# The middle outputs of a fast causal convolution, moved from VectorE to GpSimd

## The chip, the cores and the metric

The kernel runs on one core of a Trainium2 chip. The metric is the device time of one execution in microseconds (us); the kernel before takes 746.35 us, the median of two runs (746.24 and 746.46). The engines are TensorE (PE; PEld is its weight load), VectorE (DVE), ScalarE (ACT), GpSimd (POOL) and the queue engine SyncE (SP). Each runs its own list of instructions in order, and they wait for one another through semaphores.

## The reference

```python
# x: (8, 4096, 512) f32, kernel: (8, 512, 512) f32
out = zeros_like(x)
for k in range(8):
    # shifted: x moved k places later along the sequence, zeros ahead
    out += matmul(shifted(x, k), kernel[k])
```

It is a causal convolution along the sequence with 8 taps, and each tap is a 512 x 512 matrix.

## The kernel before

The 8 x 4096 positions are cut into 128 runs of 256 positions, one run to a partition row. Position t of all 128 runs is one block of 128 x 512. Of each run the first four positions (HEAD) are computed directly; the remaining 252 are worked off in 21 steps (NB) of 12 positions (STEP). A step is a fast convolution: instead of all products of 8 taps with 12 positions, sums and differences of rows of x are multiplied by sums and differences of the taps, and the products are recombined. The outermost recombination has four nodes in each step, in this order: PL, MI, H1 and H0. Each node goes through one slot of the loop, and has two halves, b = 0 (LO) and b = 1 (HI), each of which is a pair of PSUM banks p[b] holding two blocks of 128 x 512 f32.

What a node needs, with the names in the code:

- VectorE makes the sums of rows in bf16, all from SBUF to SBUF: Z from XR (`node_z`), A from Z (`node_A`), S from Z (`node_s`) and F from S (`node_F`, acts F0 and F1). They are the weights that TensorE loads for its products (L117).
- ScalarE seeds the banks from an earlier product (`node_seed`, acts s0 and s1; L187, L189), copies a product (`node_a1`, L168 and L171) and makes DT (L193).
- VectorE subtracts within the pairs of banks (`node_d`, acts d0 and d1; L81 and L206), with one operand in PSUM and DT in SBUF.
- TensorE's products come in acts a1 or b1 (weights A or Z), a0, u, v0 and v1 (weights S), l00 to l11 (weights F, or S for a leaf). Only H0 (and one early node) is a leaf, and a leaf has no F and no d0 or d1.

The outputs are made in `node_e` (acts e0 and e1, one for each half). In the PL slot ScalarE takes half of PL out of PSUM into a tile cc[b] in SBUF (L229). In the MI slot VectorE makes dd[b] = cc[b] - MI/2 (L232). In the H1 slot it makes y = H1 + dd[b] (L236), and stores it; in the H0 slot dd[b] = dd[b] - H0 (L243, in place), and stores that. The middle outputs are made in `middle` (act g0 in the H1 slot, act g1 in the H0 slot): cc[b] = 2 cc[b] - dd[b], in place, on VectorE (L247), and stored.

The order of all this is written out by hand. After the ramp, each slot plays a list of acts, in which "nxt" and "two" nodes ahead are prepared beside the current one:

```python
PL: "s l00 F1 a0 l01 u l11 e0 s0 z s1 v0 F0 A x dt d0 v1 d1 l10 a1 e1",
MI: "s l01 l00 F1 a0 u l11 e0 s0 z s1 dt A F0 v0 x v1 d1 l10 d0 e1 a1",
H1: "s l00 F1 a0 l01 u l11 s0 dt e0 z s1 A F0 g0 v0 d0 r v1 d1 l10 e1",
H0: "s l00 F1 b1 l01 a0 u e0 l11 s0 z s1 dt F0 A v0 x d0 g1 v1 d1 l10 a1 e1",
```

So in the H1 slot VectorE does S (of H0), F1, e0, Z, A (of PL), g0, e1, and in the H0 slot S (of PL), e0, Z, F0, A, d0 (of PL), g1, d1, e1.

The tiles cc, dd and y come from one pool of five buffers of 128 x 1024 f32, each free again once its store has landed (or its last reader is through). In the loop cc[0] always takes the buffer of the step before's cc[0], dd[0] that of the step before's dd[0], and the two H1 outputs of one step share a buffer one after the other.

SyncE issues the stores of the outputs (L218) and the transposing loads (L94). GpSimd issues the loads of x rows (L87), three to a step in act r of the H1 slot; ahead of them it copies two elements of A into a tile junk (`behind`, L106), so that they don't go out before VectorE has made A.

Of the kernel before, what the change touches and what calls it, by code (L numbers as in the profile page):

```python
# [14 lines left out]
def kernel(  # L15
# [6 lines left out]
    nc = tc.nc  # L22
# [11 lines left out]
    ADD = mybir.AluOpType.add  # L34
    SUB = mybir.AluOpType.subtract
    MUL = mybir.AluOpType.mult
# [32 lines left out]
    DT = spool.tile([P, D], f32, name="DT")  # L69
# [7 lines left out]
    H, zero = WP[:, 0:8], DT.bitcast(bf)[:, 0:D]  # L77
    xin = {0: W[MI, MID, MID], 4: W[MI, MID, HI], 8: W[MI, MID, LO]}

    def tt(o, a, b, op):  # L80
        nc.vector.tensor_tensor(out=o, in0=a, in1=b, op=op)  # L81

    def pair(k):
        return ppool.tile([P, 2, D], f32, name=f"pp{k}")
# [43 lines left out]
    def zsum(o, t0, t1, n, op):  # L128
        done = 0
        while done < n:  # L130
            p0, p1 = place(t0 + done), place(t1 + done)
            m = min(n - done, R - p0, R - p1)
            tt(Z[:, o + done:o + done + m], XR[:, p0:p0 + m], XR[:, p1:p1 + m], op)
            done += m
# [12 lines left out]
    def node_A(n):  # L147
        tt(AX[n.k % 2], n.z[:, n.o + 2:n.o + 4], n.z[:, n.o + 3:n.o + 5], ADD)

    def node_s(n):  # L150
        tt(SX[n.k % 2], n.z[:, n.o:n.o + 5], n.z[:, n.o + 2:n.o + 7], ADD)
# [47 lines left out]
    def node_d(n, b_):  # L199
        if n.leaf:  # L200
            return
        p = n.p[b_]
        if b_ == LO:
            tt(p[:, 0], DT, p[:, 1], SUB)
        else:
            nc.vector.scalar_tensor_tensor(out=p[:, 0], in0=p[:, 1], scalar=-1.0,  # L206
                                           in1=DT, op0=MUL, op1=SUB)

    def node_l(n, b_, j):
        o = n.p[b_][:, j]  # L210
# [6 lines left out]
    def store(t, y):  # L217
        nc.sync.dma_start(out=orr[:, t:t + 2, :], in_=y)  # L218

    cc, dd = {}, {}  # L220

    def y_tile():
        return ypool.tile([P, 2, D], f32, name="y")

    def node_e(n, b_):
        p, t = n.p[b_], n.t + 2 * b_
        if n.a == PL:
            cc[b_] = y_tile()
            nc.scalar.mul(out=cc[b_], in_=p, mul=0.5)  # L229
        elif n.a == MI:  # L230
            dd[b_] = y_tile()
            nc.vector.scalar_tensor_tensor(out=dd[b_], in0=p, scalar=-0.5,  # L232
                                           in1=cc[b_], op0=MUL, op1=ADD)
        elif n.a == H1:
            y = y_tile()
            tt(y, p, dd[b_], ADD)  # L236
            store(t, y)
        elif n.k == len(nodes) - 1 and b_ == HI:
            for j, eng in enumerate((nc.scalar, nc.sync)):
                tt(dd[b_][:, j], dd[b_][:, j], p[:, j], SUB)  # L240
                eng.dma_start(out=orr[:, t + 8 + j, :], in_=dd[b_][:, j])
        else:
            tt(dd[b_], dd[b_], p, SUB)  # L243
            store(t + 8, dd[b_])

    def middle(n, b_):
        nc.vector.scalar_tensor_tensor(out=cc[b_], in0=cc[b_], scalar=2.0,  # L247
                                       in1=dd[b_], op0=MUL, op1=SUB)
        store(n.t + 4 + 2 * b_, cc[b_])

    def load_w(tap):
# [86 lines left out]
    def step(k):  # L338
# [11 lines left out]
        def rows_ahead():  # L350
# [13 lines left out]
            "dt": (nxt, lambda: node_dts(nxt)),  # L364
            "v0": (nxt, lambda: node_v(nxt, 0)), "v1": (nxt, lambda: node_v(nxt, 1)),
            "d0": (nxt, lambda: node_d(nxt, 0)), "d1": (nxt, lambda: node_d(nxt, 1)),
            "e0": (cur, lambda: node_e(cur, 0)), "e1": (cur, lambda: node_e(cur, 1)),
            "x": (cur, moves), "r": (cur, rows_ahead), "g0": (cur, lambda: middle(cur, 0)), "g1": (cur, lambda: middle(cur, 1)),
        }
        return acts  # L370
# [127 lines left out]
    direct_out(1)  # L498
    node_A(nodes[2])
    node_d(nodes[1], 0)  # L500
    go(2, "v0")
    node_a1(nodes[2])
    wsum(MI, MID, LO)
    wsum(MI, MID, MID)
    load_x(20)
    go(1, "l00")
    node_d(nodes[1], 1)
    go(1, "l01")
    go(1, "e0")
# [119 lines left out]
```

## Time and profile before

| What | Value |
|---|---|
| median of two runs | 746.35 us (746.24, 746.46) |
| span of the profiled execution (first to last instruction) | 744.5 us |
| TensorE busy, clock | 729.4 us (98%), granted clock 1.000 |
| VectorE busy | 694.6 us (93%) |
| ScalarE busy | 241.3 us (32%) |
| GpSimd busy | 57.4 us (8%) |
| middle outputs on VectorE (L247) | 42 instructions of 1216 ns, 51.1 us |
| output stores (SyncE) | 127 of 512 KB, median 7.5 us from issue to landing |

The median lies 1.85 us above the span: that much lies around it. Times in the rows of the trace are in microseconds from the start of the span. A row has its start, its length, the engine, the line of the kernel, the operation, what it writes and reads, and in square brackets how long the engine stood idle ahead of it and what ended that. "pp" is a pair of PSUM banks. A row of VectorE or ScalarE overlaps the next one by some 0.08 us. Line L81 is a helper that many operations share; they are told apart by the tiles.

### The profile page before, as it was taken

What the parts mean: (1) busy time and instruction counts of PE and PEld (TensorE: products, weight loads), DVE (VectorE), ACT (ScalarE), POOL (GpSimd) and SP (SyncE); (2) the same over time, 40 slices, a digit from 0 to 9 for tenths busy, and PEclk for the clock granted to TensorE, in tenths of its full rate; (3) what the DMA queues carried; (4) which work ended last, traced back from release to release, by engine and by line L of the source; (5) the groups of instructions that cost most, each with busy time, mean ns of one, the idle gap of its engine ahead of it and who ended that gap; (6) DMA issues with size and microseconds to landing.
All of it is one profiled execution on the core that took longest, in us unless ns stands there. A gap on an engine that the chain in (4) does not pass through costs nothing.

```text
span 744.5 us, 8887 instructions
## 1 busy us (share of the span) xinstructions
PE 729.4 (98%) x3362; PEld 331.6 (45%) x3430; DVE 694.6 (93%) x725; ACT 241.3 (32%) x368; POOL 57.4 (8%) x98
## 2 busy tenths in 40 slices
PE   8989999999999999999999999999999999999997
PEld 4434444444444444444444444444444444444443
DVE  1989999999999999999999999999999999999996
ACT  3053333332333333232323323242333323333331
POOL 4200010101010010101011010101101010100000
PEclk9999999999999999999999999999999999999999
DMA  9994979696886969697795969678595968865314
GB/s 202 210 208 134 227 152 246 138 237 160 199 208 160 247 136 241 148 219 185 183 233 136 246 141 234 170 178 238 138 242 137 248 156 189 220 148 194 124 78 170
DMA packets 159371, 138.88 MB, mean 187 GB/s; under 512 B 130144, under 2 KB 134240, under 8 KB 159200
## 3 DMA queue, kind: packets, MB, share of 16 engines
q1 hardware_dynamic: 145456, 99.89, 49.5%
q0 software_dynamic: 13728, 38.15, 28.0%
q8 instruction: 27, 0.44, 0.3%
q10 hardware_dynamic: 144, 0.26, 0.1%
q14 instruction: 16, 0.13, 0.0%
HBM read 77.33 MB, written 99.09 MB: 237 GB/s over the span
## 4 chain that ended last, share of the span: by engine, by line
PE 89%; DVE 4%; issue 1%; ACT 1%; DVEq 0%; ACTq 0%
PE pp L117 89%; DVE Z L81 1%; DVE y L81 1%; DVE S L81 0%; DVE w L81 0%; DVE y L247 0%; DVE A L81 0%; DVE pp L81 0%; DVE F L81 0%; ACT pp L187 0%; ACT pp L168 0%; ACT y L229 0%; ACT pp L189 0%; DVEq L624 0%; DVEq L81 0%
## 5 line engine op out<-in xcount | busy, mean ns | idle before, releaser
L117 PE MATMUL pp<-w,S 128*128 128x512 bf16 x1175 | 274.3, 379 | 1.3
L117 PE MATMUL pp<-w,F 128*128 128x512 bf16 x970 | 244.9, 379 | 1.1
L117 PEld LDWEIGHTS <-S 128*128 128x128 bf16 x1200 | 117.1, 98 | 142.9 <-issue 3.4
L117 PE MATMUL pp<-w,A 128*128 128x512 bf16 x661 | 170.6, 379 | 2.8 <-ACT pp L189 1.2
L81 DVE TENSOR_TENSOR Z<-XR 128x2048 bf16<-128x2048 bf16 (+3 forms) x109 | 154.2, 1432 | 0.1
L117 PEld LDWEIGHTS <-F 128*128 128x128 bf16 x992 | 97.0, 98 | 117.1
L81 DVE TENSOR_TENSOR S<-Z 128x2560 bf16<-128x2560 bf16 (+1 forms) x85 | 124.3, 1464 | 0.0
L187 ACT COPY pp<-pp 128x512 f32<-128x512 f32 (+1 forms) x84 | 57.8, 688 | 154.8 <-PE pp L117 152.0
L117 PEld LDWEIGHTS <-A 128*128 128x128 bf16 x672 | 65.2, 97 | 83.2 <-DVE A L81 4.4
L171 ACT COPY pp<-pp 128x512 f32<-128x512 f32 x62 | 35.3, 570 | 197.1 <-PE pp L117 197.1
L117 PE MATMUL pp<-w,Z 128*128 128x512 bf16 x330 | 85.4, 379 | 0.3
L81 DVE TENSOR_TENSOR F<-S 128x1024 bf16<-128x1024 bf16 x124 | 84.5, 682 | 0.0
L106 POOL COPY junk<-A 128x2 bf16<-128x2 bf16 x18 | 17.6, 977 | 557.6 <-DVE A L81 557.6
L189 ACT ACTIVATE pp<-pp 128x512 f32<-128x512 f32 (+1 forms) x84 | 58.6, 698 | 5.4 <-DVE y L232 2.8
L232 DVE SCALAR_TENSOR_TENSOR y<-pp,y 128x1024 f32<-128x1024 f32 x42 | 51.3, 1220 | 9.4 <-PE pp L117 9.0
L81 DVE TENSOR_TENSOR A<-Z 128x1024 bf16<-128x1024 bf16 x84 | 57.7, 686 | 1.4
L229 ACT ACTIVATE y<-pp 128x1024 f32<-128x1024 f32 x42 | 43.1, 1027 | 42.1 <-PE pp L117 40.1
L206 DVE SCALAR_TENSOR_TENSOR pp<-pp,DT 128x512 f32<-128x512 f32 x62 | 42.9, 692 | 14.3 <-PE pp L117 13.6
L81 DVE TENSOR_TENSOR y<-pp,y 128x1024 f32<-128x1024 f32 x42 | 51.1, 1216 | 1.8 <-DMA out_dram<-y 1.6
L81 DVE TENSOR_TENSOR y<-y,pp 128x1024 f32<-128x1024 f32 (+1 forms) x43 | 50.9, 1185 | 2.0 <-PE pp L117 2.0
L247 DVE SCALAR_TENSOR_TENSOR y<-y 128x1024 f32<-128x1024 f32 x42 | 51.1, 1216 | 0.0
L117 PEld LDWEIGHTS <-Z 128*128 128x128 bf16 x336 | 32.8, 98 | 39.7 <-DVE w L81 0.3
(28 smaller groups left out, 241.3 us busy)
## 6 DMA issues: line engine op xcount, KB each, us to landing
out_dram<-y SPq DMA_DIRECT2D x127, 512.0 KB, 7.5
xd<-in_x_dram POOLq DMA_DIRECT2D x61, 512.0 KB, 10.8
w<-in_kernel_dram POOLq DMA_DIRECT2D x8, 512.0 KB, 15.8
w<-in_x_dram SPq DMA_DIRECT2D x1, 1024.0 KB, 4.8
w<-in_x_dram POOLq DMA_DIRECT2D x2, 512.0 KB, 13.5
XR<-xd SPq DMA_TRANSPOSE x61, 5.0
w<-in_x_dram POOLq DMA_DIRECT2D x2, 256.0 KB, 18.5
w<-in_x_dram POOLq DMA_DIRECT2D x1, 384.0 KB, 20.1
```

The lines of the kernel that those rows point to most:

```text
L81: nc.vector.tensor_tensor(out=o, in0=a, in1=b, op=op)
L106: nc.gpsimd.tensor_copy(out=junk, in_=z[:, 0:2])
L117: nc.tensor.matmul(bank, lhsT=comp[:, c * P:(c + 1) * P], rhs=w[:, c, :], start=start and c == 0, stop=c == DC - 1, skip_group_check=True)
L171: nc.scalar.copy(out=n.q[:, 0], in_=n.q[:, 1])
L187: nc.scalar.copy(out=o, in_=q)
L189: nc.scalar.mul(out=o, in_=q, mul=-1.0)
L206: nc.vector.scalar_tensor_tensor(out=p[:, 0], in0=p[:, 1], scalar=-1.0, in1=DT, op0=MUL, op1=SUB)
L229: nc.scalar.mul(out=cc[b_], in_=p, mul=0.5)
L232: nc.vector.scalar_tensor_tensor(out=dd[b_], in0=p, scalar=-0.5, in1=cc[b_], op0=MUL, op1=ADD)
L247: nc.vector.scalar_tensor_tensor(out=cc[b_], in0=cc[b_], scalar=2.0, in1=dd[b_], op0=MUL, op1=SUB)
```

## The change

The middle outputs go to GpSimd as a plain add. So that an add is enough, the tiles hold other multiples: cc is PL itself (ScalarE copies instead of halving), and dd is (MI - PL)/2, made in two instructions: ScalarE writes -cc/2 into dd, and VectorE adds MI/2 to it from PSUM. The signs in the H1 and H0 outputs are turned to suit. The helper `tt` and a new one, `stt`, keep the last VectorE instruction that they recorded, and the add on GpSimd is given a dependency on it: it doesn't start before that instruction is through. In the list of the H1 slot that instruction is A, and in the H0 slot it is d0. The store of each middle output follows the add; GpSimd's own list then has the add of g0 ahead of the junk copy and the three loads of act r.

```diff
+    last = {}
+
     def tt(o, a, b, op):
-        nc.vector.tensor_tensor(out=o, in0=a, in1=b, op=op)
+        last["dve"] = nc.vector.tensor_tensor(out=o, in0=a, in1=b, op=op)
+
+    def stt(o, a, by, b, op):
+        last["dve"] = nc.vector.scalar_tensor_tensor(out=o, in0=a, scalar=by, in1=b, op0=MUL, op1=op)
...
-            nc.vector.scalar_tensor_tensor(out=p[:, 0], in0=p[:, 1], scalar=-1.0,
-                                           in1=DT, op0=MUL, op1=SUB)
+            stt(p[:, 0], p[:, 1], -1.0, DT, SUB)
...
         if n.a == PL:
             cc[b_] = y_tile()
-            nc.scalar.mul(out=cc[b_], in_=p, mul=0.5)
+            nc.scalar.copy(out=cc[b_], in_=p)
         elif n.a == MI:
             dd[b_] = y_tile()
-            nc.vector.scalar_tensor_tensor(out=dd[b_], in0=p, scalar=-0.5,
-                                           in1=cc[b_], op0=MUL, op1=ADD)
+            nc.scalar.mul(out=dd[b_], in_=cc[b_], mul=-0.5)
+            stt(dd[b_], p, 0.5, dd[b_], ADD)
         elif n.a == H1:
             y = y_tile()
-            tt(y, p, dd[b_], ADD)
+            tt(y, p, dd[b_], SUB)
             store(t, y)
         elif n.k == len(nodes) - 1 and b_ == HI:
             for j, eng in enumerate((nc.scalar, nc.sync)):
-                tt(dd[b_][:, j], dd[b_][:, j], p[:, j], SUB)
+                stt(dd[b_][:, j], dd[b_][:, j], -1.0, p[:, j], SUB)
                 eng.dma_start(out=orr[:, t + 8 + j, :], in_=dd[b_][:, j])
         else:
-            tt(dd[b_], dd[b_], p, SUB)
+            stt(dd[b_], dd[b_], -1.0, p, SUB)
             store(t + 8, dd[b_])
 
     def middle(n, b_):
-        nc.vector.scalar_tensor_tensor(out=cc[b_], in0=cc[b_], scalar=2.0,
-                                       in1=dd[b_], op0=MUL, op1=SUB)
+        i = nc.gpsimd.tensor_tensor(out=cc[b_], in0=cc[b_], in1=dd[b_], op=ADD)
+        tc.add_manual_dep(i.ins, last["dve"].ins.name,
+                          mybir.DependencyInfo(mybir.DependencyClass.Sync, mybir.DependencyReason.DATA),
+                          reason="behind")
         store(n.t + 4 + 2 * b_, cc[b_])
```

## The prediction

> **What bounds the kernel now.** I read the page's shares first, then the busy time by stage, then one period of the main loop engine by engine.
>
> ```profile
> span 744.5 us, 8887 instructions
> ...
> PE 729.4 (98%) x3362; PEld 331.6 (45%) x3430; DVE 694.6 (93%) x725; ACT 241.3 (32%) x368; POOL 57.4 (8%) x98
> ...
> PEclk9999999999999999999999999999999999999999
> ```
> ```profile
> 100.00:150.00 50.00, 49.79 (x229) 22.56 (x231) 47.93 (x49) 15.49 (x24) 5.03 (x8) 1.00 0.76 179
> ```
>
> In the second fence, the busy time by stage, the columns are the stage, its length, then busy PE, PEld, DVE, ACT, POOL, then clock and DMA. TensorE is busy 99.5% of the loop at full clock: between 100 and 700 us it idles under 3 us in all. So the 51.1 us that VectorE spends on the 42 middle outputs (L247, 1216 ns each) are beside the path. Work taken off VectorE can win only TensorE's gaps, some 4 us with those of 50 to 100 us. It can lose much more, because VectorE has little slack. The timeline of one period (a step of 12 outputs, 32.9 us) shows where:
>
> ```profile
> 305.86 0.69 DVE L81 TENSOR_TENSOR A<-Z 128x1024 bf16<-128x1024 bf16 x1
> ...
> 306.47 1.22 DVE L247 SCALAR_TENSOR_TENSOR y<-y 128x1024 f32<-128x1024 f32 x1
> 306.60 0.66 PEld L117 LDWEIGHTS <-A 128*128 128x128 bf16 x4 [0.21 <-DVE A L81]
> ...
> 307.60 1.22 DVE L81 TENSOR_TENSOR y<-pp,y 128x1024 f32<-128x1024 f32 x1
> ...
> 308.74 1.48 DVE L81 TENSOR_TENSOR S<-Z 128x2560 bf16<-128x2560 bf16 x1
> ...
> 314.41 0.69 DVE L81 TENSOR_TENSOR pp<-DT,pp 128x512 f32<-128x512 f32 x1
> 315.00 1.22 DVE L247 SCALAR_TENSOR_TENSOR y<-y 128x1024 f32<-128x1024 f32 x1
> ...
> 316.74 1.21 DVE L81 TENSOR_TENSOR y<-y,pp 128x1024 f32<-128x1024 f32 x1
> ...
> 319.27 0.68 DVE L81 TENSOR_TENSOR F<-S 128x1024 bf16<-128x1024 bf16 x1
> ...
> 320.34 0.74 PEld L117 LDWEIGHTS <-F 128*128 128x128 bf16 x4
> 320.55 1.03 PE L117 MATMUL pp<-w,F 128*128 128x512 bf16 x4
> ```
>
> Two deadlines stand here. A of the next PL node ends at 306.55, and TensorE's weight load, which wanted it 0.21 earlier, starts 0.05 later: no slack at all. From there VectorE runs without a gap through H1 and H0 to F1 of PL, which ends at 319.95. Its weight load must start 0.13 ahead of the matmul, as at A (306.60 for 306.73), so by 320.42: with 0.05 for the signal the slack is 0.42 us. After that VectorE waits for TensorE twice, in the MI slot:
>
> ```profile
> 326.83 1.23 DVE L232 SCALAR_TENSOR_TENSOR y<-pp,y 128x1024 f32<-128x1024 f32 x1 [0.47 <-PE pp L117]
> ...
> 331.23 0.70 DVE L206 SCALAR_TENSOR_TENSOR pp<-pp,DT 128x512 f32<-128x512 f32 x1 [0.71 <-PE pp L117]
> ```
>
> So the chain starts afresh each period, and what makes F1 later than 0.42 us stops TensorE once a period.
>
> **Off VectorE.** Each period loses 1.13 us of L247 in the H1 slot (306.47 to 307.60) and 1.14 in the H0 slot. The changed signs (PL kept whole, MI minus PL halved) leave the H1 and H0 outputs one VectorE instruction each, with the same operands, so the rows of 1216 and 1209 ns stay.
>
> **Onto ScalarE.** The 42 new half products read and write SBUF; the nearest rows are L229's 1027 ns and the 1045 ns cast, so 1.0 us each. The 42 us fit in ScalarE's 503 idle ones. The second of a step stands behind DT (ends 330.19) and is done by 331.2, before VectorE wants it at 332.43. The first stands behind PL's second copy (325.64, 1.03 long), so it ends near 327.6, and the MI output, which now waits for it, starts at 327.65 instead of the 326.83 of the first row above. Without its 0.71 wait the L206 row would have started at 330.43; 0.82 later is 331.25 against 331.23. The wait on TensorE thus hides all but 0.02, or all but 0.12 if the product takes 1.1. I take 0.03, which A passes on to TensorE, having no slack; without that cover it would be 0.8 a period. The seed of the same pair of banks (ScalarE, 329.09) comes after the delayed reader's end (328.87).
>
> **Onto GpSimd: the length of an add.** No row has a 1024-element add on GpSimd. Its rows are: a set of 1 element 98 ns, of 128 elements 204, a select that reads and writes 128 elements 287. Writing costs (204-98)/127 = 0.83 ns an element, reading (287-204)/128 = 0.65. Two reads and a write are 2.13, so 1024 elements take 2.18 + 0.10 = 2.28 us, which I take. From below, the second read free: 1.6. From above, the select's price twice: 3.1.
>
> The Trainium skill speaks against the move: GPSIMD Engine Reference, section 3.1, gives 4497 ns for an f32 add of 2048 elements, twice VectorE's time, and advises VectorE for elementwise work. No row here has such an add; by half that figure (2.25 us, an estimate) the sum below would end at 761.3.
>
> **Onto GpSimd: who holds whom.** The copy into junk (2 elements) shows it. Each time it becomes due just after A:
>
> ```profile
> 76.22 0.18 POOL L106 COPY junk<-A 128x2 bf16<-128x2 bf16 x1 [39.88 <-DVE A L81]
> ...
> 339.64 1.05 POOL L106 COPY junk<-A 128x2 bf16<-128x2 bf16 x1 [30.44 <-DVE A L81]
> ```
> ```profile
> 76.08 1.21 DVE L81 TENSOR_TENSOR y<-pp,y 128x1024 f32<-128x1024 f32 x1
> ...
> 339.42 1.22 DVE L247 SCALAR_TENSOR_TENSOR y<-y 128x1024 f32<-128x1024 f32 x1
> ```
>
> Beside an operation with one operand in PSUM it takes 0.18 us. Beside L247, with both inputs in SBUF, it lasts until 340.69, when L247 (to 340.64) is through. So an operation with two SBUF inputs shuts GpSimd out to its end. I take the reverse as well: VectorE's next sum of two SBUF inputs waits for GpSimd's add. No row of before shows that direction.
>
> The Trainium skill (SBUF — State Buffer, Who interferes with whom) states both directions: whichever of the two issues second is blocked until the first ends. By the rule the sum is the forecast's; by the direction alone that the rows show it is the first rival's.
>
> **The sum.** H1 slot: the add starts 0.14 after A (339.50 to 339.64 in the rows), 306.69, and ends at 308.97. VectorE meanwhile does the e1 output on PSUM (306.47 to 307.7; it reuses the buffer of the e0 output, whose store was issued at 303.92 and landed in 2.6, at 306.5). S must wait to 309.02, against 308.74: +0.28, though an operation has gone. H0 slot: d0 ends at 315.10 + 0.28 = 315.38, the add runs from 315.52 to 317.80. The held-back start does not save VectorE here: e1 of H0 overwrites the MI tile which that add reads, and so stands behind it, with S, F1 and all the rest of VectorE queued after. With 0.1 for the signal (0.05 and 0.14 are the rows) e1 starts at 317.90 instead of 316.74: +1.16. F1 is ready at 319.95 + 1.16 + 0.05 = 321.16 against 320.42, so TensorE stops for 0.74; with A's 0.03 it is 0.77 us a period. Each 0.1 us of the add counts twice.
>
> There are 21 steps, hence 20 passages from H0 to a next PL: 15.4 us. In the tail the last add runs from 737.79 + 0.14 to 740.21 and holds the last two half outputs (740.03 before) by 0.3; its 512 KB store falls later and in front of theirs, some 0.4: +0.7. GpSimd's own queue: behind g0 stand junk and three loads of 0.52 us, late by 4 us at most (add, then S), but done by 313, before g1; they fetch rows two steps ahead, so nothing waits. SP's queue: the g0 store goes 1.4 later, ahead of e1's; at their landing times of 3.5 to 10.2 the buffer is free by 319.4, and ScalarE takes it at 319.89. Sum: 744.5 + 16.1 = 760.6 for the span; the median of 746.35 lies 1.85 above the span, so 762.5.
>
> **Rivals.** (1) Not slower: VectorE isn't held by GpSimd. The place is S in the H1 slot: it starts at 307.7, and d0 is then bound by TensorE's v0 (near 313.86, 0.55 before 314.41). e1 comes at +1.16 - 0.28 - 0.55 = +0.33, under the 0.42 of slack, so F1 is in time; 0.6 (A's 0.03 twenty times) and 0.7 of tail give 747.7. It decides once S starts before 308.2. For it: nothing shows the reverse direction. Against it: the full stop in the rows. With the hold but an add of 1.6 us the lateness also vanishes: 747.7. (2) Worse: operations with one PSUM operand hold the add too, so that g0 starts behind e1 (1.13) and g1 behind d1 (0.6): 0.77 + 1.73 = 2.5 a period, 797. The 0.18 us row is against it. An add of 3.1 us would give 0.77 + 1.64 = 2.41, so 795. (3) The store of g0 takes 12.6 us (the longest here): the PL copy is held to 321.8, the seed behind it, which has no slack before its matmul (321.38 for 321.45), by 1.9; 1.1 a period more than the 0.77, 785. (4) The freed VectorE closes TensorE's gaps, the 4 us above: 742.4 at best; A's deadline lies ahead of both removed operations, which speaks against any gain.
>
> **How the numbers follow.** The forecast, hold and an add of 2.1 to 2.45 us: 0.57, by itself 755 to 770. Rival 1 with the short add: 0.26. Worse: 0.09. Store: 0.05. Gain: 0.03. The range from 747 to 782 leaves out at most the last three, 0.17. About 2% is what a measurement of this kernel tells from no change, 15 us: above 761.3 lie 0.36 of the forecast's 0.57, and the 0.14 of worse and store: 0.50. No case reaches 731: 0.01. The rest, 0.49, is within 2%.
>
> **What would show it.** Right: adds of near 2.3 us starting 0.1 to 0.2 after A and d0; S of the H1 slot starting as the add ends; e1 of H0 waiting about 1.5 us for GpSimd; one TensorE wait on F a period of 0.7, and VectorE busy near 645. Wrong: S beside the add, a TensorE wait elsewhere (A, a seed), or none.

## The result

The changed kernel takes 764.59 us (median of 764.37 and 764.80) against 746.35 before: 1.0244 times as long, with a 95% interval of 1.0215 to 1.0274. It is slower by 18.2 us, where 16.1 were forecast (762.5 us).

The page of the changed kernel, its busy times and the chain of work that ended last:

```profile
span 762.6 us, 9081 instructions
...
PE 737.2 (97%) x3430; PEld 330.1 (43%) x3430; DVE 673.8 (88%) x683; ACT 281.2 (37%) x410; POOL 163.2 (21%) x140
...
DVE 48%; PE 32%; POOL 7%; issue 5%; DMA 1%; POOLq 0%; ACT 0%; DVEq 0%; SPq 0%
```

VectorE has 20.8 us less busy time and the kernel takes 18 us longer. The last line is the best pointer on the page: before, that chain was TensorE's for 89% of the span; now it runs through VectorE for 48% and GpSimd for 7%. VectorE's busy share fell, and yet the chain went over to it. (The busy time fell by 20.8 us and not by the 51.1 of L247. Of the difference of 30 us, 25 are in the S and Z rows, 147.1 and 156.4 us now, 124.3 and 154.2 before: a VectorE instruction that GpSimd holds counts as busy.)

The timeline of the changed kernel, in the period that answers to the one shown of before. L83 and L86 are VectorE's two helpers, L251 is the add, L122 the product, L111 the junk copy:

```profile
313.91 0.69 DVE L83 TENSOR_TENSOR A<-Z 128x1024 bf16<-128x1024 bf16 x1
...
314.68 1.23 DVE L83 TENSOR_TENSOR y<-pp,y 128x1024 f32<-128x1024 f32 x1
314.76 1.03 PE L122 MATMUL pp<-w,A 128*128 128x512 bf16 x4
314.83 2.36 POOL L251 TENSOR_TENSOR y<-y 128x1024 f32<-128x1024 f32 x1 [22.42 <-DVE A L83]
...
315.82 2.72 DVE L83 TENSOR_TENSOR S<-Z 128x2560 bf16<-128x2560 bf16 x1
...
317.13 1.45 POOL L111 COPY junk<-A 128x2 bf16<-128x2 bf16 x1
```
```profile
322.73 0.68 DVE L83 TENSOR_TENSOR pp<-DT,pp 128x512 f32<-128x512 f32 x1
323.33 0.68 DVE L86 SCALAR_TENSOR_TENSOR pp<-pp,DT 128x512 f32<-128x512 f32 x1
325.87 1.22 DVE L86 SCALAR_TENSOR_TENSOR y<-y,pp 128x1024 f32<-128x1024 f32 x1 [1.86 <-POOL y L251]
327.01 1.49 DVE L83 TENSOR_TENSOR S<-Z 128x2560 bf16<-128x2560 bf16 x1
328.41 0.69 DVE L83 TENSOR_TENSOR F<-S 128x1024 bf16<-128x1024 bf16 x1
```
```profile
323.49 2.34 POOL L251 TENSOR_TENSOR y<-y 128x1024 f32<-128x1024 f32 x1 [3.42 <-DVE pp L83]
```
```profile
327.72 1.03 PE L122 MATMUL pp<-w,Z 128*128 128x512 bf16 x4
...
329.15 0.55 PEld L122 LDWEIGHTS <-F 128*128 128x128 bf16 x4 [0.90 <-DVE F L83]
329.15 1.04 PE L122 MATMUL pp<-w,F 128*128 128x512 bf16 x4 [0.41 <-DVE F L83]
```

The reader is to see four things. S of the H1 slot lasts 2.72 us instead of 1.48: it is issued at 315.82, the add ends at 317.19, and S ends 1.35 after that, at 318.54. Its "busy" time holds a stop. The junk copy behind the add then lasts to 318.58, S's end: the same stop in the other direction. In the H0 slot e1 stands idle for 1.86 us and starts 0.04 after the second add. And TensorE's products with F start 0.05 after F1 ends (329.10), having waited: a group of four products that doesn't wait starts 0.86 after the one ahead of it (in the trace of before 319.69 and 320.55), so this one was due at 328.58 and is 0.57 late. (Its row has 0.41, because the row ahead is drawn 1.03 long.)

From A's end to F1's end before took 13.40 us, now 14.50: 0.27 more up to S's end in the H1 slot (3.67 from A's end before, 3.94 now), 0.82 more between d0's end and e1's start (1.64 before, 2.46 now). The period went from 32.89 to 33.49 us (17 periods, by the starts of A).

Where the 18.1 us of span came in can be followed by comparing one VectorE instruction that both traces have, A of PL, step by step:

| Up to | before | after | lost so far |
|---|---|---|---|
| A of step 4's PL | 141.41 | 146.45 | 5.04 |
| A of step 21's PL, 17 periods on | 700.54 | 715.73 | 15.19 |
| end of the last matmul | 739.93 | 755.36 | 15.43 |
| end of the span | 744.5 | 762.6 | 18.1 |

So 5.0 us belong to the first steps, 10.15 to 17 periods (0.60 each), and 2.7 come after the last matmul.

### The profile page after: what moved, and what is told of

It is laid out like the page before. It is cut to its first block, busy times and chain, and to the rows that moved or that the text cites. A ratio compares the mean times of both kernels' runs of the same rounds, so it can differ in the third digit from the quotient of the medians.

```text
span 762.6 us, 9081 instructions
## 1 busy us (share of the span) xinstructions
PE 737.2 (97%) x3430; PEld 330.1 (43%) x3430; DVE 673.8 (88%) x683; ACT 281.2 (37%) x410; POOL 163.2 (21%) x140
## 4 chain that ended last, share of the span: by engine, by line
DVE 48%; PE 32%; POOL 7%; issue 5%; DMA 1%; POOLq 0%; ACT 0%; DVEq 0%; SPq 0%
PE pp L122 32%; DVE S L83 12%; DVE Z L83 10%; DVE y L86 10%; POOL y L251 7%; DVE y L83 6%; DVE F L83 4%; DVE A L83 3%; DVE pp L83 2%; DMA out_dram<-y 1%; DVE w L83 1%; POOLq L630 0%; SPq L99 0%; ACT y L233 0%; DVE pp L86 0%
## 5 line engine op out<-in xcount | busy, mean ns | idle before, releaser
L122 PE MATMUL pp<-w,S 128*128 128x512 bf16 x1200 | 276.4, 379 | 0.6 <-ACT pp L192 0.6
L122 PE MATMUL pp<-w,F 128*128 128x512 bf16 x992 | 247.6, 379 | 10.4 <-DVE F L83 10.4
L251 POOL TENSOR_TENSOR y<-y 128x1024 f32<-128x1024 f32 x42 | 99.4, 2366 | 574.0 <-DVE A L83 414.8
L122 PEld LDWEIGHTS <-S 128*128 128x128 bf16 x1200 | 117.2, 98 | 142.7 <-issue 0.8
L122 PE MATMUL pp<-w,A 128*128 128x512 bf16 x672 | 172.0, 379 | 3.5 <-DVE A L83 1.6
L83 DVE TENSOR_TENSOR Z<-XR 128x2048 bf16<-128x2048 bf16 (+3 forms) x109 | 156.4, 1453 | 1.7 <-DMA XR<-xd 1.6
L122 PEld LDWEIGHTS <-F 128*128 128x128 bf16 x992 | 95.4, 98 | 132.8 <-DVE F L83 20.2
L83 DVE TENSOR_TENSOR S<-Z 128x2560 bf16<-128x2560 bf16 (+1 forms) x85 | 147.1, 1732 | 0.0
L122 PEld LDWEIGHTS <-A 128*128 128x128 bf16 x672 | 65.0, 97 | 84.8 <-DVE A L83 6.8
L86 DVE SCALAR_TENSOR_TENSOR y<-y,pp 128x1024 f32<-128x1024 f32 (+1 forms) x43 | 51.1, 1190 | 40.6 <-POOL y L251 39.7
L122 PE MATMUL pp<-w,Z 128*128 128x512 bf16 x336 | 86.2, 379 | 0.0
L83 DVE TENSOR_TENSOR F<-S 128x1024 bf16<-128x1024 bf16 x124 | 84.7, 683 | 0.0
L86 DVE SCALAR_TENSOR_TENSOR y<-pp,y 128x1024 f32<-128x1024 f32 x42 | 51.3, 1221 | 15.8 <-ACT y L236 15.5
L83 DVE TENSOR_TENSOR A<-Z 128x1024 bf16<-128x1024 bf16 x84 | 57.6, 686 | 1.4
L233 ACT COPY y<-pp 128x1024 f32<-128x1024 f32 x42 | 42.7, 1016 | 42.9 <-PE pp L122 42.9
L83 DVE TENSOR_TENSOR y<-pp,y 128x1024 f32<-128x1024 f32 x42 | 51.2, 1220 | 5.9 <-DMA out_dram<-y 4.6
L122 PEld LDWEIGHTS <-Z 128*128 128x128 bf16 x336 | 32.8, 98 | 39.7 <-DVE w L83 0.3
L236 ACT ACTIVATE y<-y 128x1024 f32<-128x1024 f32 x42 | 45.0, 1071 | 0.7 <-DMA out_dram<-y 0.6
L83 DVE TENSOR_TENSOR pp<-DT,pp 128x512 f32<-128x512 f32 x62 | 42.5, 685 | 2.1 <-PE pp L122 2.1
```

Source lines behind the costliest of these rows:

```text
L83: last["dve"] = nc.vector.tensor_tensor(out=o, in0=a, in1=b, op=op)
L86: last["dve"] = nc.vector.scalar_tensor_tensor(out=o, in0=a, scalar=by, in1=b, op0=MUL, op1=op)
L122: nc.tensor.matmul(bank, lhsT=comp[:, c * P:(c + 1) * P], rhs=w[:, c, :], start=start and c == 0, stop=c == DC - 1, skip_group_check=True)
L233: nc.scalar.copy(out=cc[b_], in_=p)
L236: nc.scalar.mul(out=dd[b_], in_=cc[b_], mul=-0.5)
L251: i = nc.gpsimd.tensor_tensor(out=cc[b_], in0=cc[b_], in1=dd[b_], op=ADD)
```

## The experiments

My theory was the prediction's: an add on GpSimd and a VectorE operation with two SBUF inputs shut one another out; e1 of H0 waits for the add because it overwrites the add's input; both make F1 late, and what exceeds F1's slack stops TensorE. The rivals were that the half products on ScalarE cost, that the two adds' costs simply add up, that the hold is what costs, and that signals between the engines cost whatever the add's length. All times are medians beside the kernel before on the same chip, which took 747.03 us beside the first four and 747.17 beside the last four (single runs of it lie between 746.3 and 747.8). The losses per period come from the same 17 periods as above.

### The signs alone

```diff
-        i = nc.gpsimd.tensor_tensor(out=cc[b_], in0=cc[b_], in1=dd[b_], op=ADD)
-        tc.add_manual_dep(i.ins, last["dve"].ins.name, ...)
+        tt(cc[b_], cc[b_], dd[b_], ADD)
```

> The change without its move: the new multiples, signs and half products on ScalarE stay, and the middle outputs are plain adds on VectorE with no hold. Theory (the loss comes from the adds on GpSimd alone; the ScalarE product makes the MI output 0.81 us later, which the old wait on TensorE hides to 0.02 a period): 746.8 us, within 0.5 of before. Rival (the later MI output or the fuller ScalarE is part of the loss, a third of the 18 us or more): 752 or more.

Measured: 746.54 us, 0.9993 of before (0.9983 to 1.0002). The loss per period is -0.01 us. The half products and the later MI output cost nothing that can be measured.

### One add at a time

```diff
+        if b_ == HI:   # g0_only; LO for g1_only
+            tt(cc[b_], cc[b_], dd[b_], ADD)
+        else:
             i = nc.gpsimd.tensor_tensor(out=cc[b_], in0=cc[b_], in1=dd[b_], op=ADD)
             ...
```

> The changed kernel with g0 on GpSimd as it is and g1 back on VectorE as a plain add. Theory (the two lateness terms, +0.27 at S of the H1 slot and about +0.8 at e1 of the H0 slot, only cost what exceeds the slack of some 0.55 us at F1 of PL, so that either alone costs nothing in the loop): loop period as before (32.9 us), F1 late by 0.27 without a TensorE wait; the ramp still loses some 2.5 us, where the first add stands between two parts of Z; 749. Rival (the costs add up): about half the loss, 755.

Measured: 751.50 us, 1.0056 (1.0041 to 1.0071), with 0.04 us lost per period. S of the H1 slot is stopped as in the changed kernel, and in the loop almost nothing comes of it:

```profile
313.31 2.70 DVE L83 TENSOR_TENSOR S<-Z 128x2560 bf16<-128x2560 bf16 x1
```

The total lies between the theory's 749 and the rival's 755; the loss per period is what decides. Of the 4.5 us, 3.8 come in between the first A and that of step 4's PL (1.42 us behind before there, 5.19 here), more than the 2.5 that I had put into the ramp.

> The changed kernel with g1 on GpSimd as it is and g0 back on VectorE as a plain add ahead of e1 of H1. Theory: VectorE is then as before up to d0 of the H0 slot, e1 of H0 waits for the add, +0.83 at F1 against a slack of 0.55, so the period grows by 0.25 to 0.3 us and the total by 5 to 6 us, with 2.5 of tail and 1 of ramp: 755 us. Rival (the stop of S in the H1 slot is what costs, the wait of e1 is hidden): within 2 us of before but for the tail, 749 or less.

Measured: 756.76 us, 1.0129 (1.0112 to 1.0145), with 0.34 us lost per period against an expected 0.25 to 0.3. e1's wait as g1_only's timeline has it, unchanged from the full change:

```profile
320.19 1.22 DVE L86 SCALAR_TENSOR_TENSOR y<-y,pp 128x1024 f32<-128x1024 f32 x1 [1.85 <-POOL y L254]
```

The two halves lose 0.04 and 0.34 us a period, the whole 0.60. The remaining 0.22 is a cost of having both: the first add's 0.27 uses up slack that the second would have had. Here the cost isn't the sum of the two parts; it is what their lateness together exceeds the slack by.

### A tile of its own for e1 of H0

```diff
+        elif b_ == HI:
+            y = y_tile()
+            stt(y, dd[b_], -1.0, p, SUB)
+            store(t + 8, y)
         else:
             stt(dd[b_], dd[b_], -1.0, p, SUB)
```

> The changed kernel in which e1 of the H0 slot writes a tile of its own instead of overwriting dd, so that it needn't wait for the add of g1; both adds stay on GpSimd with their hold, and the pool keeps its five buffers. Theory: e1 runs beside the add; S behind it has two SBUF inputs and starts when the add ends, 1.2 us earlier than in the changed kernel; F1 is then late by less than 0.1 us and TensorE doesn't wait: period 32.9 us, total 746.35 plus 5 of ramp plus 2.5 of tail, 754. Rival (e1's wait is not for the overwritten tile, or what stops VectorE is the add's length whatever stands behind it): S no earlier, 764.

Measured: 752.82 us, 1.0074 (1.0059 to 1.0089), with -0.01 us lost per period. VectorE's timeline of own_tile in the H0 slot, and the add:

```profile
318.81 0.69 DVE L86 SCALAR_TENSOR_TENSOR pp<-pp,DT 128x512 f32<-128x512 f32 x1
320.04 1.22 DVE L86 SCALAR_TENSOR_TENSOR y<-y,pp 128x1024 f32<-128x1024 f32 x1 [0.54 <-PE pp L122]
321.17 1.50 DVE L83 TENSOR_TENSOR S<-Z 128x2560 bf16<-128x2560 bf16 x1
```
```profile
318.97 2.35 POOL L255 TENSOR_TENSOR y<-y 128x1024 f32<-128x1024 f32 x1 [3.42 <-DVE pp L83]
```

e1 now runs inside the add's time (it waits only for TensorE), and S is issued 0.15 us ahead of the add's end at 321.32 and loses next to nothing by it. With the wait on the overwritten tile gone the loop's whole loss is gone, though both adds are still there, as long as before, and S of the H1 slot is still stopped. So the loop's loss needs that overwriting: by itself it costs 0.34 a period (g1_only), and the stop of S, which costs next to nothing alone, brings it to 0.60.

### Without the hold

```diff
-        tc.add_manual_dep(i.ins, last["dve"].ins.name, ...)
```

> The changed kernel without the dependency that holds the adds back: each starts once its two tiles are there and GpSimd's list has come to it. Theory (an add stops the next VectorE sum of two SBUF inputs for as long as it runs, wherever it stands): the add of g0 is due right behind the MI output, gets in between Z and A of the MI slot, and makes A of PL, which has no slack, 2 us late each period, while e1's wait of 1.9 goes; 780 to 795 us. Rival (the holding back is what costs, since it puts the add of g1 right ahead of e1): 752 or less.

Measured: 795.11 us, 1.0646 (1.0625 to 1.0667), with 2.26 us lost per period (2.0 in fifteen of the 17 periods, 4.2 and 4.1 in the last two, for which no reason is shown). The timeline of no_hold, in the MI slot:

```profile
310.56 1.22 DVE L83 TENSOR_TENSOR Z<-XR 128x2048 bf16<-128x2048 bf16 x1
310.77 3.22 POOL L251 TENSOR_TENSOR y<-y 128x1024 f32<-128x1024 f32 x1 [17.43 <-issue]
...
311.81 2.73 DVE L83 TENSOR_TENSOR A<-Z 128x1024 bf16<-128x1024 bf16 x1
...
316.40 0.81 PE L122 MATMUL pp<-w,F 128*128 128x512 bf16 x3 [1.78 <-DVE pp L83]
```

The add comes due during Z, waits for Z's end at 311.78, and gets its turn between Z and A: its row ends at 313.99, 2.21 after Z. A of 0.69 us then takes 2.73. The total is at the upper end of what the theory had, but the place is another: I had named A of PL as the deadline that fails, but TensorE stops earlier, at the products of H1 that stand behind d0. The hold is worth 30 us here, so holding the adds back is right.

### Half the add

```diff
-        i = nc.gpsimd.tensor_tensor(out=cc[b_], in0=cc[b_], in1=dd[b_], op=ADD)
+        i = nc.gpsimd.tensor_tensor(out=cc[b_][:, 0], in0=cc[b_][:, 0], in1=dd[b_][:, 0], op=ADD)
```

> The changed kernel with adds of 512 elements a partition instead of 1024: the second position of each middle pair is left unadded (stored as PL). Nothing else differs, neither the order nor the waits. Theory (lateness at F1 = twice the add's length less a fixed 3.6 us, the excess over 0.55 stops TensorE): adds of 1.2 us, S of H1 not held, e1 of H0 waiting under 0.8, no TensorE wait in the loop, period 32.9; with some ramp and tail 749 us. Rival (the signals and hand-overs between GpSimd and VectorE cost, whatever the length): 757 or more.

Measured: 750.42 us, 1.0042 (1.0028 to 1.0057), with 0.03 us lost per period. The half adds take 1.27 us each, and e1 of H0 waits for TensorE, not for GpSimd:

```profile
317.66 1.27 POOL L251 TENSOR_TENSOR y<-y 128x512 f32<-128x512 f32 x1 [3.73 <-DVE pp L83]
```
```profile
319.47 1.22 DVE L86 SCALAR_TENSOR_TENSOR y<-y,pp 128x1024 f32<-128x1024 f32 x1 [1.10 <-PE pp L122]
```

Length decides: in the loop the signals by themselves cost nothing visible. Most of the 3.2 us that are left lies at the two ends: in the trace 1.5 between the first A and that of step 4's PL, and 1.65 behind the last matmul.

### The first and the last step on VectorE

```diff
+        if n.k < 5 or n.k >= len(nodes) - 4:
+            tt(cc[b_], cc[b_], dd[b_], ADD)
+        else:
             i = nc.gpsimd.tensor_tensor(out=cc[b_], in0=cc[b_], in1=dd[b_], op=ADD)
             ...
```

> The changed kernel with the middle outputs of the first and the last step on VectorE as plain adds, those of the 19 steps between on GpSimd as they are. Theory (of the 18 us some 5 are lost around the first step, where the first add stands between two parts of Z, and some 2.5 behind the last matmul, where the last add's store is late; the rest is 0.60 a period): 746.35 plus 19 times 0.6, 758 us, and the end of the span as far behind the last matmul as before. Rival (the loss is all in the periods): 763.

Measured: 758.73 us, 1.0155 (1.0140 to 1.0170). In the comparison by A, only 0.43 us are lost up to step 4 (5.04 in the changed kernel), the periods lose 0.62 each, and the span ends 4.56 us behind the last matmul, as before (4.57; in the changed kernel 7.24). So some 7 of the change's 18 us, over a third, sit at its two ends. Where the first step's loss begins can be read in the changed kernel's timeline there:

```profile
71.31 4.24 DVE L83 TENSOR_TENSOR Z<-XR 128x1536 bf16<-128x1536 bf16 x2
```
```profile
71.48 2.99 POOL L251 TENSOR_TENSOR y<-y 128x1024 f32<-128x1024 f32 x1 [41.33 <-DVE y L86]
```

The hand-written ramp puts no operation on PSUM behind g0's place. The add waits for the first part of Z, runs, and the second part waits for it: 4.24 us for the two parts, 2.08 before. As VectorE no longer has the middle output to make (1.13 us), this alone makes it about 1 us late, and there is more. Three loads of x rows stand behind this add in GpSimd's own list. Before, they went out from 32.13 us on; now they wait for the add. The three loads of act r, behind the add of g1, go out at 89.11 instead of 76.46. In the second step Z then waits for a transposing load, and TensorE's products with A wait 1.59 us behind it. GpSimd before, GpSimd in the changed kernel, and that Z:

```profile
32.13 0.52 POOL L87 DMA_DIRECT2D xd<-in_x_dram  x1 [2.03 <-DMA w<-in_kernel_dram]
34.63 0.52 POOL L87 DMA_DIRECT2D xd<-in_x_dram  x1 [1.98 <-DMA w<-in_x_dram]
35.83 0.52 POOL L87 DMA_DIRECT2D xd<-in_x_dram  x1 [0.68 <-DMA w<-in_x_dram]
```
```profile
74.42 1.55 POOL L92 DMA_DIRECT2D xd<-in_x_dram  x3
```
```profile
111.06 2.02 DVE L83 TENSOR_TENSOR Z<-XR 128x3584 bf16<-128x3584 bf16 x1 [1.65 <-DMA XR<-xd]
```

That the transposing load is late because of the late loads isn't shown. The 5.0 us aren't split up either: counted from the first A to that of step 4's PL, g0_only loses 3.8, own_tile 2.7, half_add 1.5 and g1_only 0.8.

### Both repairs

This is the tile for e1 together with the first and last step on VectorE.

> Both repairs: e1 of H0 in a tile of its own, and the first and last step's middle outputs on VectorE. Theory: nothing is late in the loop, the ramp or the tail, so the time is that of before within 1 us; and no faster, since TensorE bounds the loop, although VectorE has some 46 us less to do. Rival (a VectorE with slack lets TensorE's remaining gaps close): 743 or less.

Measured: 746.60 us, 0.9992 (0.9983 to 1.0001), with -0.02 us lost per period. All of the loss is undone, and there is no gain: from 100 to 700 us TensorE is busy for 597.05 us of 600. The page's busy line of own_tile_inner:

```profile
PE 729.6 (98%) x3362; PEld 331.4 (44%) x3430; DVE 677.0 (91%) x687; ACT 280.9 (38%) x410; POOL 153.7 (21%) x136
```

None of the versions is measurably faster than before. With TensorE at its rate throughout the loop, work moved off VectorE has next to nothing to win here.

## Why the prediction was right, and where its sum was off

**What bounds the kernel.** Right. TensorE sets the loop, and the only thing that the change could do there was miss a deadline. Without the wait on the tile (own_tile) the loop runs at the old period, and with both repairs the kernel takes the old time, not less.

**Off VectorE and onto ScalarE.** Right. The half product makes the MI output 0.81 us later, as worked out (from a1's product to that output 2.79 us before, 3.60 now), and the old wait on TensorE hides it to 0.02, where I took 0.03. The signs alone cost nothing.

**The add.** 2.36 us, where 2.28 was taken from the rows of the set and the select. Half the length takes 1.27, so 0.18 us is fixed, where 0.10 was taken, and 2.13 ns go to an element, the rate that was worked out. That the rate agrees to the last digit is partly luck: it came from single rows of two other operations on 128 elements. The prediction's estimate by half the figure of the Trainium skill (GPSIMD Engine Reference, section 3.1) was 2.25; the runs lie 0.11 above it.

**Who holds whom.** Right in both directions. The row of before showed GpSimd stopped by VectorE; the 2.72 us of S shows the reverse. The rule of the Trainium skill (SBUF — State Buffer, Who interferes with whom) agrees with it. S came 0.27 later, where 0.28 was predicted. The first rival, in which S isn't held, is out. One sign was wrong: VectorE was to be busy for near 645 us, and its rows show 673.8; most of the difference is stopped S rows, which count as busy.

**e1 of H0.** Right: its start moves by 1.09 in all, where 1.16 was predicted. It stands idle behind the add for 1.86 us; the prediction said about 1.5, but its own sum gives 1.9 (d1 through 0.6 after d0, at 315.98, and e1 at 317.90). own_tile shows that this wait is what turns the change into a loss in the loop.

**The slack of F1.** Mis-sized. I asked that F1 be ready 0.13 us ahead of the matmul, for the weight load, and so found a slack of 0.42. The trace shows TensorE going on 0.05 after F1's end, at 329.15, with its weight load at the same time in the rows. So the slack was 0.60 - 0.05 = 0.55 (0.60 from F1's end at 319.95 to the products at 320.55). That gives 1.10 - 0.55 + 0.02 = 0.57 a period, not 0.77, and 0.60 was measured. Over the 18 passages behind step 4's A the forecast had 13.9 us, and 10.4 were measured: 3.5 too high.

**The ramp.** Mis-sized the other way. I counted its passages like any other (two of 0.77, 1.5 us), and 5.0 were lost up to step 4. The list of the first step is written out apart from the loop's, and I hadn't looked where g0 falls in it. "GpSimd's own queue ... nothing waits" was worked out for the loop; in the first step three loads of x rows stand behind the add and go out some 40 us later. inner_steps puts the loss on the first step's adds: with them on VectorE 0.43 of the 5.0 are left.

**The tail.** 0.7 was forecast, 2.7 was measured behind the last matmul (7.24 against 4.57). The last two half outputs wait 0.3 as predicted. What follows the stores can be read in the closing instructions of SyncE and GpSimd, before and in the changed kernel (a row has the shortest, median and longest in ns, then the first and the last start in us):

```profile
L624 POOLq DRAIN  x3: 45/102/17828, 636.9 to 744.2; - x3
L624 SPq DRAIN  x3: 7/7/7, 743.6 to 743.9; - x3
```
```profile
L630 POOLq DRAIN  x3: 45/102/8515, 753.3 to 762.3; - x3
L630 SPq DRAIN  x3: 7/7/7, 759.8 to 762.1; - x3
```

SyncE's first DRAIN, behind the landing of the last stores, comes 3.7 us after the last matmul before and 4.5 now: the waiting and the stores together cost 0.8, close to the forecast. The other 1.9 are a term that the sum didn't have. GpSimd's longest DRAIN starts as the last add is issued (753.3) and lasts 8.5 us, to 761.8, which is 6.1 after that add's end, and the end of the program waits for it. With an add shorter by 1.08 (half_add) this DRAIN is shorter by 1.08 (7.44 us); in inner_steps it lasts 8.5 us too, but starts at 721.1 and is long over.

The errors nearly cancel: 3.5 too much in the loop, 3.5 and 2.0 too little at its two ends, for a sum 2 us short of the measured one. That the total came so close is luck; it says little about the terms, and the periods had to be counted to see it.

**The other rivals.** Operations with one operand in PSUM don't hold the add: it starts 0.23 after A's end with such an operation running beside it. The late store of g0 didn't occur: stores land in 3.6 us by the median now, and the PL copy's idle time in the loop is for TensorE's products.

## What to carry to other kernels

Before work is moved off a busy engine, look whether that engine sets the time; where another is at its rate, the move has next to nothing to win, and what it costs is found by following the next deadline of each wait that the change adds. When an operation is moved to a slower engine, list who overwrites its inputs: an in-place update that was free on one queue becomes a wait across two, and a tile of its own was worth 12 us here. Two lateness terms in front of one deadline must be taken together, less the slack once. Look also at what stands behind the moved operation in its new engine's list, and work out the first and the last step by themselves: here they had some 7 of the 18 us.

## What the runs showed of the hardware

- GpSimd gets its turn between two VectorE instructions that stand back to back: an add that comes due during Z goes in ahead of the next operation, which then lasts 2.73 us instead of 0.69 (no_hold), or makes two parts of Z take 4.24 instead of 2.08. The prediction had not reckoned with it, and it is where the first step's loss begins.
- GpSimd's closing DRAIN ends 6.1 us after the end of its last add (761.8 for 755.69 in the changed kernel; the same in half_add, with an add of half the length). An add near the end of the program can so hold up its end, though the last store has landed (759.8).
- A stopped instruction counts as busy in the profile, on both engines: the S rows with a mean of 1732 ns, the adds of 3.22 and 2.99 us, the junk copy of 1.45. Beside the unhindered rows (1.48 for S, 2.36 for an add, 0.18 for the copy) they show where the stops are.
